# Strided and backward operand reads for the matmuls of a two-layer hybrid encoder

## The chip, the cores and the metric

The kernel runs on one core of a Trainium2 chip. Its time is the device time of one execution in microseconds, and the median over several executions is given. A profile is taken of one further execution, which has a time of its own.

## The reference

Two encoder layers over 512 tokens of width 1024, in float32. Layer 0 mixes tokens by differential attention, layer 1 by a gated linear attention; both add a cross-attention into 256 memory tokens. Each layer ends in a gated feed-forward with a causal convolution of width 3 on both halves of the up projection, and this is where the change sits:

```python
def conv_ffn(h, w_up, conv_w, conv_b, w_down):
    u = h @ w_up                                   # (512, 1024) @ (1024, 5632)
    c = lax.conv_general_dilated(u, conv_w[:, None, :], window_strides=(1,),
                                 padding=[(CONV_WIDTH - 1, 0)], ...) + conv_b
    a, g = jnp.split(c, 2, axis=-1)
    return (jax.nn.silu(g) * a) @ w_down           # (512, 2816) @ (2816, 1024)
...
for i in range(DEPTH):
    x = x + concat(token_mixer(i, ...), memory_attention(...)) @ w_out[i]
    x = x + conv_ffn(rms_norm(x, ffn_norm[i]), w_up[i], ...)
```

## The kernel before

Activations lie transposed, features on the partitions and the 512 tokens along them: eight tiles of 128 x 512 (`xT`). Every large product is made of rounded float32 parts: an operand is split into `hi` (rounded to the matmul's type) and `lo` (what the rounding left), and each product is three matmuls, hi x hi, hi x lo and lo x hi, added up in one PSUM bank.

Weights come from one packed array in DRAM, `wpack`, in blocks of 128 x 1024. A piece is the weights of one step of the plan (`_pieces`): a pair of 128-column output tiles for up (`ua`), gate (`ug`), output (`o`) and down (`dn`), with up to 12 k-tiles of 256 columns each; four k-tiles make a block. Each block is loaded into one of three raw buffers on the SP queue (`load_raw`, L262), at most three ahead (`ahead`). ScalarE casts it into a `whi` buffer (L253) and VectorE subtracts to get `wlo` (L256), in `split_weights`. There are `WB` = 6 buffers of each. `weights(key)` makes the blocks of the piece that is wanted and of the one after it.

Two ways of using a block:

- `gemm` (L330 to L332), for the projections in front of the mixers: the activations are the stationary operand, 128 tokens at a time, and the weights stream past, 512 columns wide.
- `product` (L351 to L353), for the output projections, the up and gate projections and the down projections: 128 columns of a weight tile, `hi[:, blk(n)]`, are the stationary operand (loaded by LDWEIGHTS, PEld in the profile), and the 512 tokens of an activation tile stream past into a bank of 128 x 512. n is 0 or 1: the two halves of a k-tile of 256 columns.

In the feed-forward (`ffn`), the up and gate pieces alternate q by q, `up(wa, 0)`, `up(wg, 0)`, `up(wa, 1)`, `up(wg, 1)`; each result is scaled by VectorE (L1111), convolved on ScalarE and VectorE (L1113 to L1115), gated and split into `mid` tiles. The 11 q are done in two halves of 6 and 5; after each half four down pieces (12 or 10 k-tiles) add their result to `xT` (L1061).

TensorE's instructions stand in the order in which the program issues them. The order on ScalarE and VectorE is chosen by a scheduler that knows which buffers are free. Around the mixers a written script fills TensorE with waiting matmuls (`Filler`).

Of the kernel before, what the change touches and what calls it, by code (L numbers as in the profile page):

```python
# [29 lines left out]
WTILE = 1024  # L30
HALVES = (6, 5)
XS = 36
WB = 6

TOGETHER = (((0, 2), (0, 0)), ((0, 3),), ((0, 1), (1, 1)), ((1, 2), (1, 0)), ((1, 3),))
NT = 3 * len(TOGETHER)
# [93 lines left out]
def _blocks():  # L130

    out = []
    for key, name, i, ks, ranges in _pieces():
        w = sum(b - a for a, b in ranges)
        step = WTILE // w
        out.append([(name, i, ks[j:j + step], ranges, w) for j in range(0, len(ks), step)])
    return out


# [40 lines left out]
def trunk(ctx, tc, head_d, x_t, mem_t, wpack, cols_a_d, cols_d, conv_d, gate_d, rel_bias, diff_lambda, consts, onehot, out):  # L180
# [68 lines left out]
    plan, blocks, made = _pieces(), _blocks(), []  # L249
    at = [0]  # L250

    def split_weights(c, raw, hi, lo, pin=False):
        ins = A.copy(hi[:, c], raw[:, c])  # L253
        if pin:
            tc.keep_in_program_order(ins)
        V.tensor_sub(lo[:, c], raw[:, c], hi[:, c].bitcast(F32))  # L256
# [19 lines left out]
    def make_block(raws=None):  # L276
        i, n, w = order[done[0]]
        if raws is None:
            ahead()
            raw = raw_q.popleft()  # L280
        else:
            raw = raws.pop(0)
        done[0] += 1
        while len(made) <= i:
            made.append([])
        hi, lo = (wp.tile([128, WTILE], F32R, name=t, tag=t, bufs=WB) for t in ("whi", "wlo"))
        split_weights(slice(0, n * w), raw, hi, lo, i == 2)
        made[i] += [(hi[:, blk(j, w)], lo[:, blk(j, w)]) for j in range(n)]
        if raws is None:
            ahead()  # L290

# [51 lines left out]
            F.add(6 * w / 2370.0, lambda b=b, k=k: unit(b, k, k + 2))  # L343


    def product(p, parts, n, pairs, ids=None):
        ids = range(len(parts)) if ids is None else ids
        first, last = (ids[0], ids[-1]) if len(ids) == len(parts) else (0, len(parts) - 1)
        for i in ids:
            (hi, lo), (bh, bl) = parts[i], pairs[i]  # L350
            mm(p, hi[:, blk(n)], bh, start=i == first, stop=False)  # L351
            mm(p, hi[:, blk(n)], bl, start=False, stop=False)  # L352
            mm(p, lo[:, blk(n)], bh, start=False, stop=i == last)  # L353


    xT = [None] * KT
# [80 lines left out]
    with tc.tile_pool(name="ini", bufs=1) as ip, tc.manual_schedule(engines={E.Activation, E.DVE, E.Pool, E.SP}):  # L437
        idle = ip.tile([128, 512], F32, name="idle")
        rb = ip.tile([32, 6], F32, name="rb")
        oh = ip.tile([32, 640], F32, name="oh")  # L440
        bs = xtile()[:6], xtile()[:6, :128]
        lv = xtile()[:, :256]
        G.memset(idle, 0.0)
        p = bank("tp")
        for n in (512, 320):
            mm(p[:, :n], idle[:, 0:128], idle[:, :n], start=True, stop=True)


        raws = [ip.tile([128, WTILE], F32, name=f"raw{i}") for i in range(4)]
        for t in (blk(0, S // 2), blk(1, S // 2)):  # L450
            A.dma_start(raws[0][:, t], wpack[0, :, t])
        head = ip.tile([128, 32 + S], F32, name="head")
        for c in (slice(0, 32 + S // 2), slice(32 + S // 2, 32 + S)):
            load(head[:, c], head_d[:, c])
        xT[0] = head[:, 32:]
        for k in range(1, KT):
            xT[k] = xtile()
            load(xT[k], x_t[k])
            load(raws[k // 2][:, blk(k % 2, S)], wpack[k // 2, :, blk(k % 2, S)])
        load(cols_a, cols_a_d)  # L460
        at[0] = 4
        load(C[:, 384:512], consts[:, 384:512])
        load(rb, rel_bias)
        load(oh, onehot)
        second = [load_raw(raw_tile(), WTILE) for _ in range(3)]
        load(cols, cols_d)
        load(lv, diff_lambda[0].rearrange("a b -> (a b)").partition_broadcast(128))
        parts, acc, split_w = [], [None], [None]
        made.append(parts)
        done[0] = 4  # L470

        def operands(k):
            if k % 2 == 0:
                split_w[0] = [wp.tile([128, WTILE], F32R, name=n, tag=n, bufs=WB) for n in ("whi", "wlo")]
            c = blk(k % 2, S)
            hi, lo = split_w[0]
            xh[k], xl[k] = split_tiles()
            if k == 0:
                for t in (blk(0, S // 2), blk(1, S // 2)):
                    V.tensor_copy(hi[:, t], raws[0][:, t])  # L480
                V.tensor_sub(lo[:, c], raws[0][:, c], hi[:, c].bitcast(F32))
                for t in (blk(0, S // 2), blk(1, S // 2)):
                    split(xh[0][:, t], xl[0][:, t], xT[0][:, t], col(0, head))
            else:
                split(xh[k], xl[k], xT[k], col(k, head))
                split_weights(c, raws[k // 2], hi, lo)
            parts.append((hi[:, c], lo[:, c]))
            squares(xT[k], acc)

        operands(0)  # L490
        for k in range(KT):
            if k + 1 < KT:
                operands(k + 1)
            if k == 0:
                second.append(load_raw(raws[0], WTILE))
            if k == 4:
                bias_rows(rb, oh, bs)
            if k == KT - 2:
                for j in range(4):
                    if j == 3:  # L500
                        token_rsqrt("lg", acc[0], NB, r_x[:, 0])
                    make_block(second)
                weights(("qk", 0), True)
                small_vectors()
                for c in range(2):
                    load(bias_d[:, 512 * c:min(512 * c + 512, 640)], bs[c])
            hi, lo = parts[k]
            terms = (xh[k], hi), (xh[k], lo), (xl[k], hi)
            full, left, right = slice(0, S), blk(0, S // 2), blk(1, S // 2)
            todo = [(b, i, full) for b in range(NB) for i in range(3)]  # L510
            if k == 0:
                todo = [(0, 0, left), (1, 0, left), (0, 0, right), (1, 0, right)] + sorted(
                    [u for u in todo if u[:2] not in ((0, 0), (1, 0))], key=lambda u: u[1])
            for b, i, t in todo:
                xp, w = terms[i]
                mm(first[b][:, t], xp[:, blk(b)], w[:, t], start=k == 0 and i == 0 and t is not right,
                   stop=k == KT - 1 and i == 2)
# [578 lines left out]
    def ffn(pool, l, acc):  # L1096
# [3 lines left out]
            G.memset(u[:, 0:2], 0.0)  # L1100
        nu = [0]

        def up(parts, n):
            i = nu[0]
            nu[0] += 1
            p = bank("mm" if i % 4 < 2 else "sm")
            product(p, parts, n, list(zip(xh, xl)))
            return p, us[i % 4]

        def conv(p, u, j):  # L1110
# [22 lines left out]
        for half, nq in enumerate(HALVES):  # L1133
            mids = []
            for q in range(base, base + nq):
                wa = weights(("ua", l, q))
                wg = None
                for n in range(2):
                    ua = up(wa, n)
                    wg = wg or weights(("ug", l, q))  # L1140
                    ug = up(wg, n)
                    if q == 0 and n == 0:
                        row_scales(acc[0])
                    ca = conv(*ua, 2 * q + n)
                    cg = conv(*ug, 22 + 2 * q + n)
                    A.activation(cg, cg, AF.Silu)
                    V.tensor_mul(ca, ca, cg)
                    mh, ml = split_tiles() if len(mids) < 5 else split_tiles(pool, "mid", 18)
                    A.copy(mh, ca)
                    V.tensor_sub(ml, ca, mh.bitcast(F32))  # L1150
                    mids.append((mh, ml))
# [4 lines left out]
            for c in range(4):  # L1156
                pn = bank("lg"), bank("tp")
                parts = weights(("dn", l, base, c))
                for n in range(2):
                    product(pn[n], parts, n, mids)  # L1160
                for n in range(2):
                    if last and l == 1 and c == 3 and n == 1:
                        for t, queue in ((blk(0, S // 2), nc.sync), (blk(1, S // 2), nc.scalar)):
                            V.tensor_add(xT[7][:, t], xT[7][:, t], pn[n][:, t])
                            queue.dma_start(out[7, :, t], xT[7][:, t])
                        continue
                    update(2 * c + n, pn[n], (lambda k: c_attn(1, k)) if last and l == 0 else None, acc2)
                    if last and l == 0:
                        nc.sync.dma_start(xres[2 * c + n], xT[2 * c + n])
                    if last and l == 1:  # L1170
                        nc.sync.dma_start(out[2 * c + n], xT[2 * c + n])
# [89 lines left out]
```

## Time and profile before

| | |
|---|---|
| time before, median of 2 runs | 1168.97 us (1168.45 to 1169.49) |
| profiled execution, its own time | 1168.01 us |
| its span, first to last instruction | 1166.2 us |
| granted TensorE clock | 1.000 |
| TensorE matmul, busy | 1160.7 us in 5658 instructions |
| weight loads (PEld), busy | 965.3 us in 5658 |
| VectorE / ScalarE, busy | 750.9 us / 545.5 us |
| DMA | 117.68 MB, 101 GB/s |

A row of the profile names the line of the kernel, the engine, the operation, the tiles (out<-in) and their sizes, then how often, the busy time, the mean time of one in ns, and the idle time before it with what ended it. Matmuls overlap each other, so that the time of one in a row (389 ns) is longer than the distance between two.

### The profile page before, as it was taken

The numbers are of one execution on the slowest core, as the hardware profiler recorded it, in microseconds if no ns is written. First come the engines' busy times: TensorE is split into PE (matmuls) and PEld (weight loads), VectorE is DVE, ScalarE is ACT, GpSimd is POOL, SyncE is SP. The second block draws the span as 40 slices with busy tenths as digits, with TensorE's granted clock in tenths as the row PEclk, the third lists the DMA queues.
The fourth block names the chain that finished last, engine by engine and source line by source line (L and its number), as shares of the span: only waits on it lengthen the run. The fifth ranks groups of instructions, "written<-read, shape, count | busy, mean of one in ns | idle before, by whom it ended". The sixth has DMA issues, their size and how long they took to land.

```text
span 1166.2 us, 14790 instructions
## 1 busy us (share of the span) xinstructions
PE 1160.7 (100%) x5658; PEld 965.3 (83%) x5658; DVE 750.9 (64%) x1256; ACT 545.5 (47%) x951; POOL 5.0 (0%) x27
## 2 busy tenths in 40 slices
PE   9999999999999999999999999999999999999998
PEld 7888888888888888888888888988888888888887
DVE  7576778688677326677447637777876743576741
ACT  6676687555344213344437634436643421343420
POOL 0000000000000000000000000000000000000000
PEclk9999999999999999999999999999999999999999
DMA  8423242123223223222342230333232323232231
GB/s 295 158 70 99 78 141 73 63 103 130 85 90 120 83 88 124 75 91 98 120 148 68 81 108 3 110 121 109 93 123 73 98 102 108 85 114 73 89 101 45
DMA packets 39556, 117.68 MB, mean 101 GB/s; under 512 B 4703, under 2 KB 7192, under 8 KB 39486
## 3 DMA queue, kind: packets, MB, share of 16 engines
q1 hardware_dynamic: 39054, 116.35, 29.5%
q8 instruction: 44, 0.72, 0.3%
q10 hardware_dynamic: 432, 0.39, 0.1%
q14 instruction: 26, 0.21, 0.1%
HBM read 112.52 MB, written 4.21 MB: 100 GB/s over the span
## 4 chain that ended last, share of the span: by engine, by line
PE 98%; ACT 1%; DVE 1%; issue 0%; POOL 0%; DVEq 0%; POOLq 0%
PE ps_mm L352 9%; PE ps_mm L351 9%; PE ps_mm L353 9%; PE ps_sm L353 8%; PE ps_sm L352 8%; PE ps_sm L351 7%; PE ps_mm L330 6%; PE ps_mm L332 6%; PE ps_mm L331 6%; PE ps_tp L353 3%; PE ps_lg L353 3%; PE ps_lg L352 3%; PE ps_tp L352 3%; PE ps_lg L351 3%; PE ps_tp L351 3%; PE ps_tp L220 3%
## 5 line engine op out<-in xcount | busy, mean ns | idle before, releaser
L253 ACT CAST whi<-raw 128x1024 fp32r<-128x1024 f32 (+4 forms) x212 | 207.6, 986 | 245.4 <-PE ps_tp L352 120.9
L256 DVE TENSOR_TENSOR wlo<-raw,whi 128x1024 fp32r<-128x1024 f32 (+4 forms) x212 | 240.3, 1140 | 117.5 <-ACT whi L253 116.6
L351 PE MATMUL ps_mm<-xsh,whi 128*128 128x512 f32 x438 | 171.6, 392 | 0.0
L352 PE MATMUL ps_mm<-xsl,whi 128*128 128x512 f32 x438 | 170.6, 389 | 0.0
L353 PE MATMUL ps_mm<-xsh,wlo 128*128 128x512 f32 x438 | 170.5, 389 | 0.0
L351 PE MATMUL ps_sm<-xsh,whi 128*128 128x512 f32 x378 | 147.0, 389 | 0.0
L352 PE MATMUL ps_sm<-xsl,whi 128*128 128x512 f32 x378 | 147.0, 389 | 0.0
L353 PE MATMUL ps_sm<-xsh,wlo 128*128 128x512 f32 x378 | 147.0, 389 | 0.0
L330 PE MATMUL ps_mm<-whi,xsh 128*128 128x512 f32 (+2 forms) x336 | 129.1, 384 | 0.0
L332 PE MATMUL ps_mm<-whi,xsl 128*128 128x512 f32 (+2 forms) x336 | 126.1, 375 | 0.0
L331 PE MATMUL ps_mm<-wlo,xsh 128*128 128x512 f32 (+2 forms) x336 | 125.9, 375 | 0.0
L1113 ACT ACTIVATE cvo<-u,cv 128x512 f32<-128x512 f32 x88 | 71.4, 815 | 112.1 <-DVE u L1111 112.1
L352 PEld LDWEIGHTS ps_mm<-xsl,whi 128*128 128x128 f32 x438 | 82.3, 188 | 17.2 <-DVE xsl L311 0.4
L351 PEld LDWEIGHTS ps_mm<-xsh,whi 128*128 128x128 f32 x438 | 82.2, 188 | 17.1 <-issue 0.3
L353 PEld LDWEIGHTS ps_mm<-xsh,wlo 128*128 128x128 f32 x438 | 82.2, 188 | 17.1
L1114 DVE SCALAR_TENSOR_TENSOR cvo<-u,cv,cvo 128x512 f32<-128x512 f32 x88 | 65.7, 749 | 36.2 <-ACT cvo L1113 36.0
L352 PEld LDWEIGHTS ps_sm<-xsl,whi 128*128 128x128 f32 x378 | 70.9, 188 | 14.8
L351 PEld LDWEIGHTS ps_sm<-xsh,whi 128*128 128x128 f32 x378 | 70.9, 188 | 14.7
L353 PEld LDWEIGHTS ps_sm<-xsh,wlo 128*128 128x128 f32 x378 | 70.9, 188 | 14.7
L332 PEld LDWEIGHTS ps_mm<-whi,xsl 128*128 128x128 f32 x336 | 63.2, 188 | 11.6
L330 PEld LDWEIGHTS ps_mm<-whi,xsh 128*128 128x128 f32 x336 | 63.2, 188 | 11.3 <-ACT ks L659 0.3
L331 PEld LDWEIGHTS ps_mm<-wlo,xsh 128*128 128x128 f32 x336 | 63.3, 188 | 10.4
(295 smaller groups left out, 1760.1 us busy)
## 6 DMA issues: line engine op xcount, KB each, us to landing
raw<-in_wpack_dram SPq DMA_DIRECT2D x178, 512.0 KB, 3.5
xt<-in_x_t_dram SPq DMA_DIRECT2D x15, 256.0 KB, 5.2
raw<-in_wpack_dram SPq DMA_DIRECT2D x15, 256.0 KB, 3.0
raw<-in_wpack_dram SPq DMA_DIRECT2D x8, 384.0 KB, 3.0
xres<-xt SPq DMA_DIRECT2D x8, 256.0 KB, 3.0
xt<-xres SPq DMA_DIRECT2D x8, 256.0 KB, 5.4
out_dram<-xt SPq DMA_DIRECT2D x7, 256.0 KB, 2.0
bt<-bias_d SPq DMA_DIRECT2D x6, 256.0 KB, 4.1
```

The costliest lines, as they stand in the source:

```text
L220: nc.tensor.transpose(dst, src, ident[:n, :n])
L253: ins = A.copy(hi[:, c], raw[:, c])
L256: V.tensor_sub(lo[:, c], raw[:, c], hi[:, c].bitcast(F32))
L330: mm(p, sh[k][:, blk(b)], hi, start=k == 0, stop=False)
L331: mm(p, sh[k][:, blk(b)], lo, start=False, stop=False)
L332: mm(p, sl[k][:, blk(b)], hi, start=False, stop=k == KT - 1)
L351: mm(p, hi[:, blk(n)], bh, start=i == first, stop=False)
L352: mm(p, hi[:, blk(n)], bl, start=False, stop=False)
L353: mm(p, lo[:, blk(n)], bh, start=False, stop=i == last)
L1113: A.activation(c, u[:, 2:], AF.Identity, scale=cv[l][:, 2, j:j + 1], bias=cv[l][:, 3, j:j + 1])
L1114: V.scalar_tensor_tensor(c, u[:, 1:S + 1], cv[l][:, 1, j:j + 1], c, op0=ALU.mult, op1=ALU.add)
```

## The change

The permutation of a block's columns in DRAM and the view of them in SBUF go together, so that a stationary tile holds the same 128 weight columns as before and they lie 1, 2, 4 or 8 columns apart in the block. For two of the six ways, the activation tile and the PSUM bank are both addressed from the last token to the first. Up and gate pieces take their way by layer and q, and down pieces by layer and half; output projections and `gemm` stay as they were. Each block buffer becomes 64 columns longer and its contents start at one of nine offsets, 8 columns (32 bytes) apart, in turn for `whi` and `wlo`. There are five buffers instead of six.

```diff
-WB = 6
+WB = 5
+PLACES = tuple(8 * i for i in range(9))
+WAYS = ((1, 1), (2, 1), (4, 1), (2, -1), (4, -1), (8, 1))
+
+def way_of(key):
+    if key[0] in ("ua", "ug"):
+        return WAYS[(key[2] + 3 * key[1]) % 6]
+    if key[0] == "dn":
+        return WAYS[(1, 3, 2, 4)[2 * key[1] + (key[2] > 0)]]
+    return None
+
+def views(tile, ks, way):
+    g = way[0]
+    out = []
+    for k in range(ks):
+        parts = []
+        for n in range(2):
+            c = 2 * k + n
+            o = c // g * 128 * g + c % g
+            parts.append(tile[:, o:o + 127 * g + 1:g])
+        out.append(parts)
+    return out
...
+    places = cycle(PLACES)
+
+    def weight_tiles():
+        c = next(places)
+        d = next(places)
+        return [wp.tile([128, WTILE + max(PLACES)], F32R, name=n, tag=n, bufs=WB)[:, o:o + WTILE]
+                for n, o in (("whi", c), ("wlo", d))]
...
-        hi, lo = (wp.tile([128, WTILE], F32R, name=t, tag=t, bufs=WB) for t in ("whi", "wlo"))
+        hi, lo = weight_tiles()
         split_weights(slice(0, n * w), raw, hi, lo, i == 2)
-        made[i] += [(hi[:, blk(j, w)], lo[:, blk(j, w)]) for j in range(n)]
+        way = way_of(plan[i][0])
+        if way:
+            made[i] += list(zip(views(hi, n, way), views(lo, n, way)))
+        else:
+            made[i] += [(hi[:, blk(j, w)], lo[:, blk(j, w)]) for j in range(n)]
...
-    def product(p, parts, n, pairs, ids=None):
+    def product(p, parts, n, pairs, ids=None, way=None):
+        if way and way[1] < 0:
+            p, pairs = p[:, ::-1], [(bh[:, ::-1], bl[:, ::-1]) for bh, bl in pairs]
...
-            mm(p, hi[:, blk(n)], bh, start=i == first, stop=False)
-            mm(p, hi[:, blk(n)], bl, start=False, stop=False)
-            mm(p, lo[:, blk(n)], bh, start=False, stop=i == last)
+            th, tl = (t[n] if isinstance(t, list) else t[:, blk(n)] for t in (hi, lo))
+            mm(p, th, bh, start=i == first, stop=False)
+            mm(p, th, bl, start=False, stop=False)
+            mm(p, tl, bh, start=False, stop=i == last)
```

On the host, the blocks of these pieces are written through the same `views`, and the two `up` calls and the down projection pass their piece's way to `product`.

More of the change, by code (lines that the diff above doesn't have):

```diff
@@ L135, in _blocks @@
         step = WTILE // w
-        out.append([(name, i, ks[j:j + step], ranges, w) for j in range(0, len(ks), step)])
+        out.append([(name, i, ks[j:j + step], ranges, w, way_of(key)) for j in range(0, len(ks), step)])
     return out
@@ L473, in operands @@
             if k % 2 == 0:
-                split_w[0] = [wp.tile([128, WTILE], F32R, name=n, tag=n, bufs=WB) for n in ("whi", "wlo")]
+                split_w[0] = weight_tiles()
             c = blk(k % 2, S)
@@ L1101, in ffn, with up @@
         nu = [0]
-        def up(parts, n):
+        def up(parts, n, key):
             i = nu[0]
@@ L1106, in up @@
             p = bank("mm" if i % 4 < 2 else "sm")
-            product(p, parts, n, list(zip(xh, xl)))
+            product(p, parts, n, list(zip(xh, xl)), way=way_of(key))
             return p, us[i % 4]
@@ L1138, in ffn @@
                 for n in range(2):
-                    ua = up(wa, n)
+                    ua = up(wa, n, ("ua", l, q))
                     wg = wg or weights(("ug", l, q))
-                    ug = up(wg, n)
+                    ug = up(wg, n, ("ug", l, q))
                     if q == 0 and n == 0:
@@ L1159, in ffn @@
                 for n in range(2):
-                    product(pn[n], parts, n, mids)
+                    product(pn[n], parts, n, mids, way=way_of(("dn", l, base, c)))
                 for n in range(2):
@@ L1226 @@
     wpack = np.zeros((len(blocks), 128, WTILE), np.float32)
-    for i, (name, l, ks, ranges, w) in enumerate(blocks):
+    for i, (name, l, ks, ranges, w, way) in enumerate(blocks):
         t = f[name][l].reshape(-1, 128, f[name].shape[-1])[list(ks)]
         t = np.concatenate([t[:, :, a:b] for a, b in ranges], axis=-1)
-        wpack[i, :, :len(ks) * w] = t.transpose(1, 0, 2).reshape(128, -1)
+        t = t.transpose(1, 0, 2).reshape(128, -1)
+        if way:
+            u, t = t, np.empty_like(t)
+            for k, parts in enumerate(views(t, len(ks), way)):
+                for n, v in enumerate(parts):
+                    v[...] = u[:, 256 * k + 128 * n:256 * k + 128 * n + 128]
+        wpack[i, :, :len(ks) * w] = t
     go = f["gla_out_norm"][0]
```

## The prediction

> **What bounds the kernel now.** First the view of cores and the head of the page, which say which engine fills the time and at what clock.
>
> ```profile
> core 0: 1166.2 us, clock 1.000
> PE 1160.7 (100%) x5658; PEld 965.3 (83%) x5658; DVE 750.9 (64%) x1256; ACT 545.5 (47%) x951; POOL 5.0 (0%) x27
> PE 98%; ACT 1%; DVE 1%; issue 0%; POOL 0%; DVEq 0%; POOLq 0%
> ```
>
> TensorE (PE) is busy for all but 5.5 of 1166.2 us at its full clock, and 98% of the chain that ended last is its own. Nothing waits long for anything else, so only what one matmul costs, or a new wait of PE, can move the time. Busy time hides the cost of one, since matmuls overlap; the distance of starts tells it. Three stretches of the timeline (start us, us, instruction), the first in the up projection of layer 0:
>
> ```profile
> 500.02 0.39 PE L353 MATMUL ps_sm<-xsh,wlo 128*128 128x512 f32 x1
> 500.03 0.19 PEld L351 LDWEIGHTS ps_sm<-xsh,whi 128*128 128x128 f32 x1
> 500.25 0.39 PE L351 MATMUL ps_sm<-xsh,whi 128*128 128x512 f32 x1
> ...
> 513.62 0.39 PE L353 MATMUL ps_mm<-xsh,wlo 128*128 128x512 f32 x1
> ```
>
> ```profile
> 736.02 0.28 PE L330 MATMUL ps_mm<-whi,xsh 128*128 128x256 f32 x1
> ...
> 737.82 0.28 PE L330 MATMUL ps_mm<-whi,xsh 128*128 128x256 f32 x1
> ```
>
> ```profile
> 22.79 0.86 PEld L424 LDWEIGHTS ps_lg<-C,xt 128*128 128x128 f32 x7
> ```
>
> From 500.02 to 513.62 lie 60 starts (20 rounds of L351 to L353): 13.60/60 = 226.7 ns for 512 streamed columns. From 736.02 to 737.82 lie 15 (five rounds of L330 to L332): 120.0 ns for 256. The difference gives (226.7 - 120.0)/256 = 0.417 ns a column, so 512 columns stream for 213.3 ns and 13.3 ns are left over for each matmul. In the third stretch each of seven stationary loads serves one streamed column, so the loads themselves set the pace: (0.86 - 0.19)/6 = 112 ns a load. A load begins 10 ns after the start of the previous matmul and takes 190 ns, so the array has a load's pass of 112 ns to do in each 226.7 ns: the loads lie wholly beside the streams.
>
> The last look is at how much that pace varies with the addresses, in the view of line L351 (min/median/max ns):
>
> ```profile
> L351 PEld LDWEIGHTS ps_mm<-xsh,whi x438: 186/188/190, 179.2 to 1096.5; 128*128 128x128 f32 x146
> L351 PE MATMUL ps_mm<-xsh,whi x438: 389/389/534, 179.4 to 1096.7; 128*128 128x512 f32 x146
> L351 PE MATMUL ps_sm<-xsh,whi x378: 389/389/389, 219.0 to 1107.6; 128*128 128x512 f32 x189
> ```
>
> These loads take their 128 columns from eight places of twelve block buffers, against streams from 36 buffers, and all of them take 186 to 190 ns. Where a contiguous operand lies makes no difference.
>
> **The change part by part.** The program keeps the order of TensorE's instructions and adds none. What changes is how `product` (L351 to L353) reads and writes.
>
> ```profile
> 0.00:1166.30 1166.30, 461.83 (x1184) 222.25 (x1184) 1.00 0.30 101
> ```
>
> That is L351 alone (PE and load busy time with counts); with L352 and L353 these are 3552 matmuls, 3 x 1184. By the loops, 22 pairs of up and gate blocks give 96 matmuls each (2 pieces x 8 k x 2 n x 3), 2112; the down projections 2 x (288 + 240) = 1056; the output projections 384. By `way_of` (22 pairs spread 4, 4, 3, 4, 4, 3 over the six ways): stationary step 1 for 4 x 96 + 384 = 768; step 2 forward 384 + 288 = 672; step 2 backward 384 + 240 = 624; step 4 forward 288 + 288 = 576; step 4 backward 384 + 240 = 624; step 8 forward 288. So 1488 loads step by 16 or 32 bytes, 1296 by 8, and 1248 matmuls read their stream from the last column to the first and write PSUM from the last to the first. The weights are permuted on the host to match, so each array cell meets the same numbers as before.
>
> *Stationary step.* No load with a step is in this trace, so its price is bounded by what a load has to spare. If the step costs nothing: 0. If a load of step 4 or 8 needs two passes for one, 2 x 112 = 224 ns: still under 226.7, as long as loads follow each other as in the third stretch; with the 13.3 ns on top it would be 237, +10 ns x 1488 = +15 us. If instead the next stream must wait for the whole longer load, a pass of 112 ns is added to each: 112 x 1488 = +167 us. Below nothing a gain can't come from the load, which is hidden already. I take 0: the first two bounds, the nearer to the row that shows loads overlapping each other, are 0 and small. The Trainium skill speaks against me here: "SBUF — State Buffer", section Specifications (TRN2), gives SBUF 16-byte lines of which at least two hits each are needed for full bandwidth, and steps of 4 and 8 floats hit each line once; by that rule the 1488 loads would be slower, by a factor that it does not state. No run here shows it yet.
>
> *Backward streams.* No matmul in this trace runs backward. The nearest row is on VectorE, where L726 reads its bias tile from the last column to the first, beside L1111, which reads both operands forward:
>
> ```profile
> L726 DVE CUSTOM_DVE_ANT_0 xt<-ps_lg,bt 128x512 f32<-128x512 f32 x12 | 7.9, 686 | 2.6 <-PE ps_lg L719 2.6
> L1111 DVE TENSOR_TENSOR u<-ps_mm,rB 128x512 f32<-128x512 f32 x44 | 30.1, 688 | 35.9 <-PE ps_mm L353 35.8
> ```
>
> 686 against 688 ns: reading SBUF backward is free at VectorE's 1.04 ns a column ((686 - 285)/384 with the 128-column row below). TensorE goes 2.5 times as fast, and writes backward as well, so the row bounds only the good end: 0. For the bad end I take that a backward stream moves one column where a forward one moves two. A pace much under the best exists on this engine: plain f32 rows cost (326 - 280)/64 = 0.72 ns a column against (390 - 282)/256 = 0.42 for the rounded type:
>
> ```profile
> L726 DVE CUSTOM_DVE_ANT_0 xt<-ps_lg,bt 128x128 f32<-128x128 f32 x12 | 3.4, 285 | 0.0
> L760 PE MATMUL ps_sm<-vv,xt 128*128 128x128 f32 x80 | 11.0, 280 | 0.0
> L1015 PE MATMUL ps_sm<-gv,xt 128*128 128x192 f32 x32 | 7.2, 326 | 0.0
> L332 PE MATMUL ps_mm<-whi,xsl 128*128 128x512 f32 x288 | 112.4, 390 | 0.0
> L332 PE MATMUL ps_mm<-whi,xsl 128*128 128x256 f32 x32 | 9.0, 282 | 0.0
> ```
>
> Half pace adds 213.3 ns x 1248 = +266 us. I take 0, by the only row that shows a backward operand.
>
> *Offsets of 32 bytes.* 0, by the view of L351: eight places in twelve buffers cost the same.
>
> *Five block buffers for six.* ScalarE's cast (L253) of a block and VectorE's subtract (L256) now wait for the block five before it.
>
> ```profile
> L253 ACT CAST whi<-raw 128x1024 fp32r<-128x1024 f32 x178 | 186.4, 1053 | 225.4 <-PE ps_tp L352 117.3 <-PE ps_sm L352 74.7 <-PE ps_mm L352 10.7
> L256 DVE TENSOR_TENSOR wlo<-raw,whi 128x1024 fp32r<-128x1024 f32 x178 | 216.6, 1222 | 111.8 <-ACT whi L253 111.0
> ```
>
> ```profile
> 613.88 0.29 PE L332 MATMUL ps_lg<-whi,xsl 128*128 128x272 f32 x1
> ...
> 618.66 0.39 PE L330 MATMUL ps_mm<-whi,xsh 128*128 128x512 f32 x1
> ```
>
> The casts already sit 225.4 us waiting for TensorE to let a buffer go, and TensorE does not stop for it: they run ahead. I counted blocks in the plan's order against the starts of their readers. The tightest place is the start of layer 1: a block last read at 613.88 + 0.29 = 614.17 gives its buffer to one first read at 618.66. 4.5 us are left for 1.05 + 1.22 = 2.3 us of cast and subtract; everywhere in the feed-forward it is over 8. The new wait holds up what stands behind the cast on ScalarE (the evacuations at L849, the convolution at L1113), which holds up a PSUM bank for TensorE, and behind the subtract on VectorE (L1111, L1061). With the 2.2 us left over all of that is covered; the scheduler also moves some casts behind neighbours for it. The raw loads on SP go out later by as much, three blocks ahead. If the cover were gone at the five projections of layer 1, each would lose up to 2.3 us: +11. I take +0.5; a gain is excluded, a buffer less frees nothing earlier.
>
> **Sum.** The profiled execution took 1168.01 us (1166.2 of span and 1.8 around it). 1168.0 + 0 + 0 + 0 + 0.5 = 1168.5. The median of the runs, 1168.97, lies 1.0 above the profiled execution, so the forecast for a median is **1169.5 us**. Its own range is 1167 to 1195 (both small bounds, +11 and +15).
>
> **The rivals.**
>
> *Backward streams run at half pace* (slower). Place: the 1248 matmuls of ways 4 and 5 and of the second down halves. It decides as soon as TensorE or PSUM moves two columns at a time only when the second follows the first upward. For it speaks that 0.417 ns a column is far above the 1.04 of the one engine seen reading backward; against it that a reversed pair is still a pair of neighbours. 1169.5 + 266 = **1435 us**. "PSUM — Partial Sum Buffer", section Specifications (TRN2), of the Trainium skill says that any non-contiguous output slows matmuls significantly; by it this rival holds if a step of -1 counts as non-contiguous, which it does not say.
>
> *Loads with a step of 4 or 8 no longer hide* (slower). Place: 1488 loads. It decides from the point where load and gap together pass 226.7 ns; 188 + 39 do so exactly now, so a second pass of 112 ns would show in full if loads did not overlap. Against it speaks the third stretch, where they do. 1169.5 + 167 = **1336 us**.
>
> *The 13.3 ns between streams shrink* (faster). If they came from load and stream meeting at like addresses, steps would break it: at most 13.3 x 2784 stepped matmuls = 37 us, **1132 us**. Against it the rows of 256 and 512 columns carry the same 13.3 ns and no address changes it.
>
> *The change is not in the instructions.* The built program has the 1248 negative steps and the 2784 stepped loads, so this falls away.
>
> **How the numbers follow.** A measurement of this kernel tells about 2% from no change, so 1146 and 1192 divide the classes. No change with small losses 0.65; backward at half pace 0.16; stepped loads exposed 0.14; gap gone 0.04; smaller losses over 2% 0.01. Faster 0.04, same 0.65, slower 0.31. A range to 1340 takes in the second rival and leaves 0.16 above and 0.04 below: 1160 to 1340.
>
> **What would show it.** Right: in the view of L351 to L353 all matmuls still 389 ns, starts 226.7 ns apart in every pair of blocks, load and idle time together 227 ns whatever the load itself takes. Wrong by the first rival: matmuls of some 600 ns in the second down halves (starts 440 apart) and 389 in the first. Wrong by the second: starts over 300 apart where the step is 4 or 8, and none where it is 1 or 2. Wrong on the buffers: PE idle time put down to the cast or the subtract at the starts of projections in layer 1.

## The result, and the profile after

The changed kernel takes 1201.16 us (median of 2 runs, 1200.94 to 1201.39) against 1168.97 before: ratio 1.0275, with a 95% interval of 1.0231 to 1.0320. It is slower by 32 us. The forecast was no change, 1169.5 us; the time lies inside the stated range of 1160 to 1340 and above the forecast's own range of 1167 to 1195.

The profiled execution took 1200.94 us. Its view of cores, busy times and chain of work:

```profile
core 0: 1199.1 us, clock 1.000
PE 1192.2 (99%) x5658; PEld 1048.4 (87%) x5658; DVE 751.0 (63%) x1256; ACT 544.6 (45%) x951; POOL 5.0 (0%) x27
PE 97%; DVE 2%; ACT 1%; issue 0%; POOL 0%; DVEq 0%; POOLq 0%
```

The count of matmuls, the clock and the owner of the chain are as before. TensorE still never rests; its work has become longer, and the span with it, by 1199.1 - 1166.2 = 32.9 us. VectorE and ScalarE have the same busy time. So the loss is in the distance from one matmul to the next, as the prediction said any loss would be. The view of the first line of `product` (now L389; L390 and L391 follow it), min/median/max ns:

```profile
L389 PEld LDWEIGHTS ps_mm<-xsh,whi x438: 186/195/338, 181.4 to 1127.1; 128*128 128x128 f32 x146
L389 PE MATMUL ps_mm<-xsh,whi x438: 387/397/532, 181.7 to 1127.4; 128*128 128x512 f32 x146
L389 PE MATMUL ps_sm<-xsh,whi x378: 388/397/418, 222.8 to 1138.5; 128*128 128x512 f32 x189
```

Before, the loads were 186 to 190 ns and the matmuls 389, nearly without spread. Now loads reach 338 and matmuls 418 ns, and the median matmul has gained 8 ns. No matmul of the third row comes near the 600 ns that half pace would give (the 532 ns of the second row has its like in the 534 ns of before).

Three stretches of the timeline (start us, us, instruction): the output projection of layer 0, where nothing is stepped or backward and only the blocks' offsets are new; a down projection with step 2 and backward streams; and an up projection with step 8.

```profile
225.61 0.40 PE L389 MATMUL ps_mm<-mxh,whi 128*128 128x512 f32 x1
...
239.56 0.40 PE L389 MATMUL ps_mm<-mxh,whi 128*128 128x512 f32 x1
...
570.24 0.40 PE L389 MATMUL ps_tp<-xsh,whi 128*128 128x512 f32 x1
...
577.24 0.40 PE L389 MATMUL ps_lg<-xsh,whi 128*128 128x512 f32 x1
...
360.50 0.41 PE L389 MATMUL ps_mm<-xsh,whi 128*128 128x512 f32 x1
361.25 0.33 PEld L390 LDWEIGHTS ps_mm<-xsl,whi 128*128 128x128 f32 x1
...
378.89 0.41 PE L389 MATMUL ps_sm<-xsh,whi 128*128 128x512 f32 x1
```

There are 60, 30 and 75 starts from the first row of a stretch to its last: 13.95/60 = 232.5 ns, 7.00/30 = 233.3 ns and 18.39/75 = 245.2 ns, where 226.7 was the pace before. All three are slower, the first one with an untouched way of reading.

The same distance, from the start of each 512-column matmul to the next start, taken over the whole trace and grouped by what the program says of the instruction (means; the load is the median of the record):

| way | matmuls | before, ns | after, ns | load before, ns | load after, ns |
|---|---|---|---|---|---|
| `product`, step 1, forward | 768 | 229.1 | 233.6 | 188 | 188 |
| step 2, forward | 672 | 226.7 | 232.8 | 188 | 195 |
| step 4, forward | 576 | 226.7 | 236.0 | 188 | 309 |
| step 8, forward | 288 | 226.7 | 245.4 | 188 | 330 |
| step 2, backward | 624 | 226.7 | 234.0 | 188 | 195 |
| step 4, backward | 624 | 226.7 | 233.9 | 188 | 308 |
| `gemm`, weights stream | 966 | 232.5 | 236.1 | 188 | 188 |

(The means of step 1, which has the output projections in it, and of `gemm` contain the matmuls that follow an interruption; the medians of both before are 227. The mean of all of `product` before is 227.2.) Added up over 226.7 ns for each, the rows come to 7.4 us before and 38.3 us after: 30.9 of the 32.9 us. Part of the rest is a wait that was not there before, in the view of PE's waits (total us, times, longest):

```profile
PE ps_tp L243 <- DVE o L817: 1.3, 1, 1.3
PE ps_tp L484 <- POOL idle L481: 1.3, 1, 1.3
```

The second of these is in the trace of before as well, as L446; the first is new.

### The profile page after: what moved, and what is told of

The parts are those of the page before. It is cut to its first block, busy times and chain, and to the rows that moved or that the text cites. A ratio compares the mean times of both kernels' runs of the same rounds, so it can differ in the third digit from the quotient of the medians.

```text
span 1199.1 us, 14745 instructions
## 1 busy us (share of the span) xinstructions
PE 1192.2 (99%) x5658; PEld 1048.4 (87%) x5658; DVE 751.0 (63%) x1256; ACT 544.6 (45%) x951; POOL 5.0 (0%) x27
## 4 chain that ended last, share of the span: by engine, by line
PE 97%; DVE 2%; ACT 1%; issue 0%; POOL 0%; DVEq 0%; POOLq 0%
PE ps_mm L389 9%; PE ps_mm L390 9%; PE ps_mm L391 9%; PE ps_sm L389 8%; PE ps_sm L390 8%; PE ps_sm L391 8%; PE ps_mm L365 6%; PE ps_mm L366 6%; PE ps_mm L367 6%; PE ps_lg L390 3%; PE ps_tp L391 3%; PE ps_lg L391 3%; PE ps_lg L389 3%; PE ps_tp L390 3%; PE ps_tp L389 3%; PE ps_tp L243 2%
## 5 line engine op out<-in xcount | busy, mean ns | idle before, releaser
L389 PE MATMUL ps_mm<-xsh,whi 128*128 128x512 f32 x438 | 175.1, 400 | 0.0
L390 PE MATMUL ps_mm<-xsl,whi 128*128 128x512 f32 x438 | 174.0, 397 | 0.0
L391 PE MATMUL ps_mm<-xsh,wlo 128*128 128x512 f32 x438 | 173.8, 397 | 0.0
L389 PE MATMUL ps_sm<-xsh,whi 128*128 128x512 f32 x378 | 150.4, 398 | 0.0
L390 PE MATMUL ps_sm<-xsl,whi 128*128 128x512 f32 x378 | 150.3, 398 | 0.0
L391 PE MATMUL ps_sm<-xsh,wlo 128*128 128x512 f32 x378 | 150.2, 397 | 0.0
L389 PEld LDWEIGHTS ps_mm<-xsh,whi 128*128 128x128 f32 x438 | 103.7, 237 | 11.5 <-issue 0.3
L391 PEld LDWEIGHTS ps_mm<-xsh,wlo 128*128 128x128 f32 x438 | 103.6, 237 | 11.5
L390 PEld LDWEIGHTS ps_mm<-xsl,whi 128*128 128x128 f32 x438 | 103.7, 237 | 11.0
L389 PEld LDWEIGHTS ps_sm<-xsh,whi 128*128 128x128 f32 x378 | 92.4, 244 | 8.9
L390 PEld LDWEIGHTS ps_sm<-xsl,whi 128*128 128x128 f32 x378 | 92.5, 245 | 8.8
L391 PEld LDWEIGHTS ps_sm<-xsh,wlo 128*128 128x128 f32 x378 | 92.3, 244 | 8.9
```

Of the source, the lines that this page charges most:

```text
L389: mm(p, th, bh, start=i == first, stop=False)
L390: mm(p, th, bl, start=False, stop=False)
L391: mm(p, tl, bh, start=False, stop=i == last)
```

## The experiments

What could explain this result: each of the three parts (steps, backward streams, offsets) makes the matmuls that it touches slower by its own amount, and the amounts add up; or one part does it all and the others are free; or the five buffers delay the casts and TensorE pays in many small waits. All kernels keep the count and the order of TensorE's instructions. Medians and ratios are against runs of the kernel before on the same chip (1168.72, 1168.26 and 1168.17 us in the three groups).

**The parts taken apart.** Steps and backward streams without the offsets (diff against the changed kernel):

```diff
-WB = 5
-PLACES = tuple(8 * i for i in range(9))
+WB = 6
+PLACES = (0,)
```

> The changed kernel with its stationary steps and backward streams alone: six block buffers, no padding, every block at offset 0. Theory A (the offsets cost the time: steps and backward streams cost little by themselves): about 1176 us, the matmuls of step 1 back at 226 to 227 ns from start to start, backward ones too, and only steps 4 and 8 longer (+3 ns x 576, +12 ns x 288, some 5 us). Theory B (steps and backward streams cost the time, and upset the pace of all other matmuls): about 1200 us. Theory C (buffers or their pitch): 1169.

Measured: 1191.10 us, 1.0195 (1.0178 to 1.0212). Then the offsets without the ways:

```diff
 def way_of(key):
+    return None
```

> The changed kernel with the nine offsets, the padding and five buffers, but every stationary tile contiguous and every stream forward. Theory A (offsets): 1190 to 1196 us, 230 to 236 ns from start to start nearly everywhere. Theory B (steps and backward streams): 1169 to 1171. Theory C (buffers or pitch): 1190 to 1196 as well, which the next kernel tells apart.

Measured: 1192.89 us, 1.0207 (1.0192 to 1.0223). Then five buffers of the longer pitch, with every block at offset 0 and no ways:

```diff
-PLACES = tuple(8 * i for i in range(9))
+PLACES = (0,)
...
 def way_of(key):
+    return None
...
-    return [wp.tile([128, WTILE + max(PLACES)], ...
+    return [wp.tile([128, WTILE + 64], ...
```

> Five buffers with the padded pitch of 1088 columns, all blocks at offset 0, all tiles contiguous, all streams forward. Theory A: 1169 to 1170, every matmul at 226 to 227 ns in the feed-forward. Theory C (a buffer less, or buffers that begin at other multiples of 256 bytes): 1185 or more.

Measured: 1171.10 us, 1.0023 (1.0014 to 1.0033). One group of the profile's costliest ones (busy us, mean ns | idle before), in this order for the three kernels:

```profile
L389 PE MATMUL ps_sm<-xsh,whi 128*128 128x512 f32 x378 | 149.7, 396 | 0.0
L389 PEld LDWEIGHTS ps_sm<-xsh,whi 128*128 128x128 f32 x378 | 92.4, 245 | 8.5
```

```profile
L390 PE MATMUL ps_sm<-xsh,whi 128*128 128x512 f32 x378 | 148.9, 394 | 0.0
L390 PEld LDWEIGHTS ps_sm<-xsh,whi 128*128 128x128 f32 x378 | 71.0, 188 | 16.9
```

```profile
L390 PE MATMUL ps_sm<-xsh,whi 128*128 128x512 f32 x378 | 147.0, 389 | 0.0
PE ps_tp L244 <- DVE o L818: 1.3, 1, 1.3
```

The buffers are not the cause: without offsets and ways the matmuls are back at 389 ns, and buffers and pitch cost 2.4 us, 1.3 of them in the new wait (where the rest lies is not shown). It is not one part alone either: the ways cost 22.4 us by themselves, and the offsets (with the buffers) 24.2. But 22.4 + 24.2 is 46.6 and the change cost 32.2: the parts don't add up. In the second kernel the load is an untouched 188 ns and the matmul is slow all the same.

**What an offset does.** All blocks at one offset of 32 bytes, instead of nine offsets:

```diff
-PLACES = tuple(8 * i for i in range(9))
+PLACES = (8,)
...
 def way_of(key):
+    return None
...
-    return [wp.tile([128, WTILE + max(PLACES)], ...
+    return [wp.tile([128, WTILE + 64], ...
```

> As offset_zero_pitch, but every block lies at one and the same offset of 8 columns (32 bytes). If it is the variety of offsets that costs (each change between hi and lo or between blocks upsets the pace anew): 1169 to 1172. If it is that an operand does not begin at a multiple of 64 bytes or more: about 1195, as with nine offsets.

Measured: 1199.07 us, 1.0261 (1.0246 to 1.0277). A single offset is worse than the nine in turn, so it is not their variety that costs. In the timeline there are 60 starts from the first to the last of these rows:

```profile
559.73 0.40 PE L392 MATMUL ps_sm<-xsh,wlo 128*128 128x512 f32 x1
...
573.88 0.40 PE L392 MATMUL ps_tp<-xsh,wlo 128*128 128x512 f32 x1
```

14.15/60 = 235.8 ns. Over the trace `product` has a mean of 233.8 ns, and `gemm` 238.2 against 232.5 before. In `gemm` the blocks are the stream and the activations the load, so it makes no difference which of the two is the shifted one. That leaves two readings: 32 bytes is a bad place for any operand, or load and stream must begin alike. The next kernel shifts everything by 32 bytes together, in the kernel before:

```diff
+    perm.tile([128, 8], F32, name="pad")
     xs = ctx.enter_context(tc.tile_pool(name="xs", bufs=1))
```

> The kernel before with one unused tile of 32 bytes a partition ahead of all others, so that streams and stationary tiles all begin 32 bytes further on and keep their distances. If the pace depends on where load and stream lie relative to each other: 1169 us and 226.7 ns from start to start. If an operand that begins off a multiple of 64 bytes is slow by itself: about 1199, as with the constant offset of the weights alone.

Measured: 1168.74 us, 1.0004 (0.9994 to 1.0013). Then three offsets of 0, 256 and 512 bytes in turn, and one of 128 bytes for all blocks (both without ways):

```diff
-PLACES = tuple(8 * i for i in range(9))
+PLACES = (0, 64, 128)
```

> Five buffers, tiles contiguous, streams forward; blocks at three offsets 256 bytes apart (0, 256 and 512) in turn, pitch 1152 columns. If the pace repeats with 256 bytes (so the starts in offsets_only suggest: pairs at 0 and 256 of 512 run at 227 to 229 ns, those at 64, 128 or 192 at 232 to 235): 1170 to 1174. If any variety of offsets costs: 1190 or more.

```diff
-PLACES = tuple(8 * i for i in range(9))
+PLACES = (32,)
```

> As offset_const, with 32 columns (128 bytes) for 8. If 256 bytes is the period: 232 to 233 ns from start to start, 1190 to 1197 us. If a start at a multiple of 64 bytes is enough: 1171.

Measured: 1171.77 us, 1.0031 (1.0020 to 1.0042) for the offsets of 256 bytes, no more than buffers and pitch account for, and 1195.40 us, 1.0235 (1.0220 to 1.0250) for 128 bytes. The rows: the group of before's L352 in the shifted kernel; the timeline with offsets of 256 bytes, 60 starts; the group with 128 bytes.

```profile
L352 PE MATMUL ps_sm<-xsh,whi 128*128 128x512 f32 x378 | 147.0, 389 | 0.0
```

```profile
539.78 0.39 PE L391 MATMUL ps_sm<-xsl,whi 128*128 128x512 f32 x1
...
553.38 0.39 PE L391 MATMUL ps_lg<-xsl,whi 128*128 128x512 f32 x1
```

```profile
L390 PE MATMUL ps_sm<-xsh,whi 128*128 128x512 f32 x378 | 149.1, 395 | 0.0
L390 PEld LDWEIGHTS ps_sm<-xsh,whi 128*128 128x128 f32 x378 | 71.2, 188 | 16.6
```

13.60/60 = 226.7 ns with offsets of 256 bytes, and 389 ns where all is shifted; 395 with 128 bytes. So what costs a 512-column matmul here is a stationary operand and a stream that begin at different places modulo 256 bytes (differences of 32 and 128 bytes were run alone, the other multiples of 32 only in the mix of nine); a shift common to both costs nothing, and a difference of 256 or 512 bytes is none. In `product` of the kernel before, by the program, the stationary tiles begin at multiples of 512 bytes in buffers of 4096, and the streams of the up and gate projections lie in buffers of 2048, so that they never met the case. Why it is 256 bytes is not shown here.

Shorter streams do not pay. In the kernel with all blocks 32 bytes on, these are the same 16 matmuls of 256 columns that the prediction timed at 120.0 ns:

```profile
755.02 0.28 PE L366 MATMUL ps_mm<-whi,xsh 128*128 128x256 f32 x1
...
756.77 0.28 PE L366 MATMUL ps_mm<-whi,xsh 128*128 128x256 f32 x1
```

From the first to the last lie 15 starts, 1.75/15 = 116.7 ns: in this stretch the shifted operands are 3.3 ns faster (all 96 matmuls of this width, interruptions included: a mean of 121.5 against 123.7). Above the streaming time that the prediction worked out, 106.7 and 213.3 ns, that leaves 10.0 ns at 256 columns and 20.5 at 512 (by the mean of 233.8), where the kernel before had 13.3 at both. Why the shift works in opposite ways stays open.

The Trainium skill, "TensorE: Matmul & The Clock Gate", section Step-by-step: what each phase is for, says that loading the next tile's weights takes no read bandwidth from the running matmul, since each has a port of its own. These rows speak against a load without any effect on the running matmul: with the load's time unchanged at 188 ns, the distance of matmuls depends on where the load lies relative to the stream. That they share read bandwidth is not shown.

**What a backward stream does.** All 3168 matmuls of up, gate and down backward, no steps, no offsets, six buffers:

```diff
-WB = 5
-PLACES = tuple(8 * i for i in range(9))
+WB = 6
+PLACES = (0,)
...
 def way_of(key):
+    return (1, -1) if key[0] in ("ua", "ug", "dn") else None
```

> The kernel before, where all 3168 matmuls of up, gate and down read their stream and write PSUM from the last column to the first; six buffers, all tiles contiguous and at offset 0. If a backward stream has a pace of its own, whatever the load does (233.3 ns in both backward ways of ways_only): 1169 + 6.6 ns x 3168 = 1190. If the backward ways were longer only for their stationary step (step 2 forward takes 233.3 as well): 1169 to 1171. Half pace would be 1169 + 676.

Measured: 1189.22 us, 1.0182 (1.0166 to 1.0197). All 3168 stand 233.3 ns apart, 5% to 95% within 233 to 234, so a backward matmul pays 6.6 ns and 3168 of them 21 us. To see which side pays, only the reading backward, and then only the writing:

```diff
-            p, pairs = p[:, ::-1], [(bh[:, ::-1], bl[:, ::-1]) for bh, bl in pairs]
+            pairs = [(bh[:, ::-1], bl[:, ::-1]) for bh, bl in pairs]
```

> As backward_only, but the 3168 matmuls of up, gate and down read their stream backward and write PSUM forward. The part changed: the result of such a product has its tokens in reverse order, which nothing puts right. If the 6.6 ns belong to reading SBUF backward: 1190 us, 233.3 ns. If they belong to writing PSUM backward: 1169.

```diff
-            p, pairs = p[:, ::-1], [(bh[:, ::-1], bl[:, ::-1]) for bh, bl in pairs]
+            p = p[:, ::-1]
```

> The other half: streams read forward, PSUM written backward; again the tokens of such a product come out in reverse order. If the 6.6 ns belong to writing PSUM backward: 1190 us; if to reading: 1169; if each has a part, the two runs share 21 us between them.

Measured: 1189.39 us, 1.0179 (1.0164 to 1.0195) for reading, 1168.74 us, 1.0002 (0.9993 to 1.0012) for writing. The timelines of the two, 60 starts each:

```profile
559.81 0.40 PE L392 MATMUL ps_lg<-xsh,wlo 128*128 128x512 f32 x1
...
573.81 0.40 PE L392 MATMUL ps_lg<-xsh,wlo 128*128 128x512 f32 x1
```

```profile
559.84 0.39 PE L391 MATMUL ps_tp<-midl,whi 128*128 128x512 f32 x1
...
573.44 0.39 PE L391 MATMUL ps_tp<-midl,whi 128*128 128x512 f32 x1
```

14.00/60 = 233.3 ns and 13.60/60 = 226.7 ns. The whole price is in reading SBUF backward beside a forward load; PSUM takes the columns in falling order at no cost. Whether a load that is backward as well would win the pace back was not tried.

**What a step does.** Step 2 for all up, gate and down pieces, and step 8 for all up and gate pieces with down left contiguous, both forward, at offset 0 and with six buffers:

```diff
 def way_of(key):
+    return (2, 1) if key[0] in ("ua", "ug", "dn") else None
```

> Six buffers, offset 0, streams forward, every stationary tile of up, gate and down with step 2. If a step that passes 1024 bytes beside a stream of 2048 loses the common pace as a wrong offset does: 233.3 ns, 1168.5 + 6.6 x 3168 = 1190 us. If the step 2 of ways_only was slow only for what ran before it: 1169 to 1172.

```diff
 def way_of(key):
+    return (8, 1) if key[0] in ("ua", "ug") else None
```

> Six buffers, offset 0, streams forward, step 8 for all tiles of up and gate (2112 matmuls), the down projections contiguous. From the 288 of ways_only (244.5 ns, loads of 331 ns): 1168.5 + 17.8 x 2112 = 1206 us. If the whole longer load showed (188 to 331 ns, +143): 1470. If step 8 was slow only by its neighbours: 1170 to 1183.

Measured: 1190.36 us, 1.0189 (1.0172 to 1.0206) for step 2; 1207.02 us, 1.0331 (1.0316 to 1.0347) for step 8. The groups of step 2, then the timeline of step 8, in an up projection and in the untouched down projection of the same kernel:

```profile
L390 PE MATMUL ps_sm<-xsh,whi 128*128 128x512 f32 x378 | 148.8, 394 | 0.0
L390 PEld LDWEIGHTS ps_sm<-xsh,whi 128*128 128x128 f32 x378 | 72.8, 193 | 15.2
```

```profile
299.71 0.41 PE L390 MATMUL ps_mm<-xsh,whi 128*128 128x512 f32 x1
299.71 0.33 PEld L391 LDWEIGHTS ps_mm<-xsl,whi 128*128 128x128 f32 x1
299.95 0.41 PE L391 MATMUL ps_mm<-xsl,whi 128*128 128x512 f32 x1
...
314.39 0.41 PE L390 MATMUL ps_sm<-xsh,whi 128*128 128x512 f32 x1
...
394.69 0.39 PE L391 MATMUL ps_tp<-xsl,whi 128*128 128x512 f32 x1
...
408.29 0.39 PE L391 MATMUL ps_lg<-midl,whi 128*128 128x512 f32 x1
```

From 299.71 to 314.39 lie 60 starts, 244.7 ns each; from 394.69 to 408.29 also 60, 226.7 ns each: the price stays with the stepped matmuls. All 3168 of step 2 stand at 233.3 ns though their load grew by 5 ns only. With step 8 the load takes 331 ns (median), 143 more, and the distance grows by 18. The load of L391 begins at 299.71 and its record ends at 300.04, after its own matmul has started at 299.95: over the 2112 the record reaches 88 ns past that start on average. Most of the longer load is thus hidden: by the records it runs beside the matmul before and into its own.

**Why the parts don't add up.** With the ways alone, the backward matmuls stand 233.4 (step 2) and 233.3 ns (step 4) apart, the forward ones of step 2 at 233.3, of step 4 at 235.0, of step 8 at 244.5. In the changed kernel, with the offsets on top, the table above has 234.0, 233.9, 232.8, 236.0 and 245.4. A matmul that has lost the common pace by one cause loses at most 1 ns more by the offset. So the offsets' new cost falls on step 1 (229.2 to 233.6) and on `gemm` (232.7 to 236.1): (4.4 x 768 + 3.4 x 966) = 6.7 us, and with the 2.4 of the buffers 9.1 of the 10.1 us that lie between 1191.10 and 1201.16.

## Why the prediction was wrong

*What bounds the kernel* held: PE alone sets the time, its idle time grew only from 5.5 to 6.9 us, and the distance of starts is the number that moved. The counts of the six ways agree with the trace, row by row.

*"Offsets of 32 bytes. 0"* was wrong, and the furthest off: offsets and buffers cost 24.2 us by themselves, the buffers 2.4 of them. The failing step is the reading of one view: "eight places in twelve buffers cost the same" was taken as "where a contiguous operand lies makes no difference". All of those places were multiples of 512 bytes (128 columns of 4 bytes) in buffers of 4096, and the streams lay in buffers of 2048, so the view held no other case. (It also held six block buffers and not twelve: L351 reads `whi` alone.) The step should have had a bound. *The 13.3 ns between streams shrink* fell with steps, which lengthen the distance to 233.3 ns and more; but the reason held against it, that no address changes the 13.3 ns, was wrong as well: one offset of 32 bytes made them 20.5 at 512 columns and 10.0 at 256.

*"Backward streams"* at 0 was wrong by 6.6 ns a matmul, 1248 x 6.6 = 8 us if alone. The VectorE row did not carry over to TensorE. The rival of half pace was much further off: starts 233 ns apart, not 440. Its second reason, the writes, has no cost that these runs can tell: the rule of "PSUM — Partial Sum Buffer" that was quoted there, if a step of -1 counts as non-contiguous, is not borne out (1.0002).

*"Stationary step"* at 0 was wrong, and its middle bound, +10 ns for steps of 4 and 8, was close to the mark: +8 to +9 forward for step 4 and +18 for step 8. It assumed a load of two passes, and the record did grow from 188 to 309 and 330 ns. That a step of 2 costs nothing failed: +6.6 ns with a load of 193. The rival of exposed loads (a pass of 112 ns in full) fell, since loads overlap the matmul behind them, as the third stretch of before had suggested. The rule that was quoted from the Trainium skill, "SBUF — State Buffer", section Specifications (TRN2), two hits in each 16-byte line, fits the loads' records: step 2 has two hits and takes 193 ns, step 4 one and takes 309. The matmuls' distance does not follow it: step 2 pays nearly what step 4 pays.

*"Five block buffers"* at +0.5 was mis-sized: 2.4 us with the longer pitch, inside its bound of 11. The one wait found, 1.3 us, is at the transposes of the mixer's output (L243), not at the projections of layer 1 where the tightest place was counted.

*The sum* put three zeros side by side, each the good end of what was known, though all three parts touch the same pace of load and stream. The own range of 1167 to 1195 took in +15 for the steps and +11 for the buffers and nothing for the offsets. Of the chance of 0.31 for slower, 0.30 lay on two mechanisms that did not happen; what did happen, smaller losses over 2%, had 0.01. That 1201.16 us lies between 1160 and 1340 is luck: the range reached so far up for the exposed loads (1336), and those did not occur.

## What to carry to other kernels

Where loads and streams follow each other on TensorE without a gap, and the streams are 512 columns wide, keep stationary tile and moving tile at the same place modulo 256 bytes, both contiguous and both forward; here any departure cost 4 to 9 ns of 227 for each matmul, a step of 8 floats 18, and a second departure almost nothing more. At 256 columns an offset of 32 bytes cost nothing (116.7 against 120.0 ns), so measure before carrying the rule to another width. When a view shows that a cost does not vary, ask first which values it contains: addresses that are all multiples of one number say nothing of the others. A record that gets much longer (a load, 188 to 330 ns) need not be paid, and one that hardly changes (188 to 193) can be the sign of a slower pace; read the distance of starts.

## What the runs showed of the hardware

- The pace of a 512-column matmul with a load beside it is 226.7 ns when both begin alike modulo 256 bytes, and 231 to 236 ns otherwise, with loads of the same 188 ns; it comes whether the load (`product`) or the stream (`gemm`) is the shifted one. At 256 columns a shift of 32 bytes gives 116.7 ns against 120.0.
- Step 2 and a backward read lead to the same 233.3 ns. The 6.6 ns are 16 columns at 0.417 ns, and the 13.3 ns left over before were 32. Whether the two have one cause stays open.
- Writing PSUM from the last column to the first costs nothing that these runs can tell (1168.74 against 1168.17 us; 1.0002, 0.9993 to 1.0012).
- Loads of 128 columns take 188, 193, 309 and 330 ns at steps of 1, 2, 4 and 8 floats, and a long one reaches 88 ns past the start of its own matmul.
